# Pinning the VectorE instructions of the ten fast pairs to the order in which the kernel writes them

## The chip, the cores and the metric

One core of one Trainium2 chip runs the whole kernel. The metric is device time in microseconds, lower is better. The profile is one execution seen by the hardware profiler. TensorE is PE (its weight loads PEld), VectorE is DVE, ScalarE is ACT, GpSimd is POOL, SyncE is SP.

## The reference

A trunk of two layers is applied to a prompt (256 tokens) and a sample (512 tokens). Each layer has two SwiGLU blocks around a mixer:

```python
def swiglu_ffn(x, w_gate, w_up, w_down):
    return (jax.nn.silu(x @ w_gate) * (x @ w_up)) @ w_down
...
    def trunk(x):
        for l in range(DEPTH):
            x = layer_norm(ALPHA * x + 0.5 * swiglu_ffn(x, ffn1_w_gate[l], ffn1_w_up[l], ffn1_w_down[l]),
                           ln1_g[l], ln1_b[l])
            mix = hybrid_mixer(x, w_in[l], conv_w[l], conv_b[l], dt_bias[l], a_log[l], d_skip[l],
                               ssm_norm_g[l], attn_norm_g[l], rpb[l], w_out[l])
            x = layer_norm(ALPHA * x + mix, ln2_g[l], ln2_b[l])
            x = layer_norm(ALPHA * x + 0.5 * swiglu_ffn(x, ffn2_w_gate[l], ffn2_w_up[l], ffn2_w_down[l]),
                           ln3_g[l], ln3_b[l])
        return x
```

The model width is 1024, the inner width of the SwiGLU is 2816, and both groups together have 768 tokens. The four SwiGLU blocks are what this change touches.

## The kernel before

**Precision.** Every number is held as a high and a low part, and a product is three matmuls per contraction step: high by high, high by low of x, low by high. The high part of a weight block is a ScalarE cast. The low part is made in one of two ways (`parts`, L91). Without `acc`, VectorE subtracts (L106). With `acc`, ScalarE writes the negated high part (L102) and a DMA issued by GpSimd adds the raw weights onto it (L103); this is the *accumulate* below.

**Pairs and slots.** The inner width is worked off in eleven pairs of 256 columns. Pair 0 is plain. Pairs 1 to 10 are the *fast pairs* (`fast_pair`, L518): gate and up are each computed with seven block products in place of eight, so a pair has fourteen slots, numbered 0 to 13 (0 to 6 gate, 7 to 13 up). Slot i runs block product i (twelve matmuls of 384 columns, L524), and it uses *weight block* i, which is a raw quarter of the weights or a sum of quarters (L89, VectorE). Weight blocks are made four slots ahead, in five tiles `w0` to `w4` taken in turn, so that block i's tile is free again when product i-5 has ended. In pairs 2 to 9, blocks 0, 1, 5, 7 and 8 come by the accumulate.

**Down products.** The down projection of the pair before is spread over slots 1 to 11: three thirds of the tokens, each with seven products of three matmuls of 512 columns (L596) in the order h0, h1, h3, h4, h6, h5, h2 (names of the tiles of the hidden values; `h3h` is a high part, `h3l` a low part). h0, h4, h5, h2 of a third share a PSUM bank psB and h1, h3, h6 two banks psC. After each product VectorE adds the bank onto the result (L599), and the next product in that bank has to wait for it. At the end of a pair VectorE combines the four hidden blocks (L445 to L448) and makes h3l to h6l (L436).

**Down weights.** In slots 8 to 13 (`down_step`) the pair's own down weights are made: steps T1, T3 (slot 9), T2 (slot 11) and -T4 (slot 12) overwrite raw quarters on VectorE (L126, L128, L130, L132), and their high and low parts go to `w5` to `w11`. T2 in slot 11 yields `w8`, -T4 yields `w11`, both through the accumulate.

**Loads.** Raw weights come in halves of 512 KB on SP's queue (L71), six for each pair: gate, gate, up, up, down, down. There are four buffers `wraw`. A load is written into the program where a half is finished with (`done`), and its instruction waits on SP until the buffer that it was given is free.

**What sets the order.** When the program is built, a scheduler places each engine's instructions: an instruction may stand ahead of one that was written earlier on the same engine where the scheduler takes it as ready sooner, and a buffer is handed out in the order in which it takes buffers to come free. On the chip each engine then works its list from top to bottom.

## Time and profile before

| | |
|---|---|
| time, three runs | 2982.32 us median (2973.87 to 2982.59) |
| profiled execution | 2994.69 us, span 2992.5 us |
| PE busy | 2883.1 us (96% of the span) |
| PEld busy | 2534.0 us (85%) |
| DVE busy | 2191.0 us (73%) |
| ACT busy | 1583.4 us (53%) |
| POOL busy | 408.8 us (14%) |
| granted TensorE clock, mean | 0.978 of full speed |

Busy shares are means over the span. The fast pairs of the four SwiGLU blocks stand at 61.7 to 514.8, 1017.5 to 1466.9, 1556.0 to 2005.6 and 2506.0 to 2951.8 us. In each, the first, second and last pair are shaped differently from the seven in the middle (the first and the last have no down products, and the pair before the second has none), so the seven *middle pairs* of each block, 28 in all, are spoken of by themselves.

### The profile page before, as it was taken

To read this page: it belongs to the slowest core of one execution; us is meant where nothing else is said; L and a number is where in the kernel's file an instruction comes from. 1 tells how busy PE (TensorE), PEld (TensorE's weight loads), DVE (VectorE), ACT (ScalarE), POOL (GpSimd) and SP (SyncE) were. 2 spreads that over 40 slices of the span, in tenths; PEclk is the share of its full clock that TensorE was granted. 3 is DMA by queue.
4 is the path that set the end of the run, shared out by engine and by line. 5 is a ranking of instruction groups with operands and counts; after the bars stand their busy time and mean duration, and the time that the engine had idled before them with its cause. 6 is when DMAs were issued, how large, how long until landed. Compare 5 with 4: busy or idle time off the path is not lost.

```text
span 2992.5 us, 41957 instructions
## 1 busy us (share of the span) xinstructions
PE 2883.1 (96%) x15094; PEld 2534.0 (85%) x15094; DVE 2191.0 (73%) x4207; ACT 1583.4 (53%) x3231; POOL 408.8 (14%) x513
## 2 busy tenths in 40 slices
PE   8999999999999999999989999999999999999998
PEld 7988889888767888888979888898887778888897
DVE  7777777768435877777797778877783458887877
ACT  4645454657345455554545455545573464554543
POOL 2112120100000211121031121200000002121210
PEclk9999999999889999999999999999997999999999
DMA  3555453224323255554215554632343233454642
GB/s 122 126 121 126 114 127 114 99 88 137 111 62 125 81 134 110 128 128 112 85 36 122 125 126 114 140 100 102 99 124 114 76 122 92 113 132 109 135 106 77
DMA packets 128880, 330.26 MB, mean 110 GB/s; under 512 B 14816, under 2 KB 27296, under 8 KB 127904
## 3 DMA queue, kind: packets, MB, share of 16 engines
q1 hardware_dynamic: 82592, 243.68, 25.6%
q0 software_dynamic: 46080, 83.91, 16.4%
q8 instruction: 118, 1.93, 0.3%
q14 instruction: 90, 0.74, 0.1%
HBM read 224.67 MB, written 18.97 MB: 81 GB/s over the span
## 4 chain that ended last, share of the span: by engine, by line
PE 71%; DVE 11%; DMA 7%; issue 6%; POOL 3%; ACT 2%; POOLq 0%; DVEq 0%; SPq 0%; ACTq 0%
PE psA L524 28%; PE psB L596 7%; PE psA L1119 5%; PE psA L407 5%; PE psA L965 5%; PE psC L596 4%; DMA w<-wraw 4%; DMA wraw<-in_w_gu_dram 3%; PE psB L1054 3%; PE psB L618 3%; PE psC L618 3%; PE psA L772 2%; PE psA L992 2%; DVE arena L599 2%; PE psC L1083 2%
## 5 line engine op out<-in xcount | busy, mean ns | idle before, releaser
L524 PE MATMUL psA<-XH,w 128*128 128x384 f32 x2560 | 700.4, 338 | 5.3 <-DMA w<-wraw 5.3
L524 PEld LDWEIGHTS psA<-XH,w 128*128 128x128 f32 x2560 | 468.6, 188 | 14.4 <-DMA w<-wraw 6.6
L103 POOL DMA_DIRECT2D w<-wraw x320 | 273.8, 881 | 1322.9 <-ACT w L102 1168.0
L524 PE MATMUL psA<-XL,w 128*128 128x384 f32 x1280 | 432.6, 338 | 0.0
L105 ACT CAST w<-arena 128x512 fp32r<-128x512 f32 x320 | 198.4, 620 | 390.2 <-PE psA L524 357.4
L105 ACT CAST w<-wraw 128x512 fp32r<-128x512 f32 (+1 forms) x320 | 194.6, 620 | 214.4 <-PE psA L524 103.9
L106 DVE TENSOR_TENSOR w<-wraw,w 128x512 fp32r<-128x512 f32 (+1 forms) x320 | 216.0, 688 | 110.1 <-ACT w L105 106.3
L599 DVE SCALAR_TENSOR_TENSOR arena<-psB,arena 128x512 f32<-128x512 f32 x384 | 260.7, 686 | 45.5 <-PE psB L596 45.5
L106 DVE TENSOR_TENSOR w<-arena,w 128x512 fp32r<-128x512 f32 x320 | 219.6, 687 | 66.4 <-ACT w L105 66.4
L524 PEld LDWEIGHTS psA<-XL,w 128*128 128x128 f32 x1280 | 240.7, 188 | 7.5
L101 ACT CAST w<-wraw 128x512 fp32r<-128x512 f32 x320 | 197.4, 618 | 92.8 <-PE psA L524 56.5
L407 PE MATMUL psA<-XH,w 128*128 128x256 f32 (+1 forms) x1056 | 241.5, 335 | 5.0 <-DVE XH L372 5.0
L102 ACT ACTIVATE w<-w 128x512 fp32r<-128x512 f32 x320 | 198.8, 631 | 5.7
L599 DVE SCALAR_TENSOR_TENSOR arena<-psC,arena 128x512 f32<-128x512 f32 x288 | 191.7, 684 | 3.3
L407 PEld LDWEIGHTS psA<-XH,w 128*128 128x128 f32 x1056 | 168.6, 189 | 27.0 <-DVE XH L372 6.3
L524 PE MATMUL psA<-T4h,w 128*128 128x384 f32 x640 | 183.6, 348 | 0.0
L524 PE MATMUL psA<-T3h,w 128*128 128x384 f32 x640 | 181.1, 344 | 0.0
L524 PE MATMUL psA<-T2h,w 128*128 128x384 f32 x640 | 177.4, 338 | 0.0
L89 DVE TENSOR_TENSOR arena<-wraw 128x512 f32<-128x512 f32 x160 | 109.4, 686 | 91.9 <-DMA wraw<-in_w_gu_dram 81.6
L539 DVE TENSOR_TENSOR arena<-arena,psA 128x384 f32<-128x384 f32 x240 | 132.0, 550 | 56.9 <-PE psA L524 50.3
L330 POOL TENSOR_TENSOR stat<-stat,cst 128x1 f32<-128x1 f32 x60 | 25.7, 429 | 1033.2 <-ACT arena L933 415.7
L407 PE MATMUL psA<-XL,w 128*128 128x256 f32 (+1 forms) x528 | 151.1, 335 | 2.0 <-DVE XL L373 2.0
(359 smaller groups left out, 6356.0 us busy)
## 6 DMA issues: line engine op xcount, KB each, us to landing
wraw<-in_w_gu_dram SPq DMA_DIRECT2D x176, 512.0 KB, 3.8
w<-wraw POOLq DMA_DIRECT2D x320, 256.0 KB, 4.1
wraw<-in_w_dn_dram SPq DMA_DIRECT2D x88, 512.0 KB, 3.7
e<-ac_d SPq DMA_DIRECT2D x48, 256.0 KB, 3.3
wraw<-in_w_xbc_dram SPq DMA_DIRECT2D x16, 512.0 KB, 4.7
wraw<-in_w_qk_dram SPq DMA_DIRECT2D x16, 512.0 KB, 3.9
arena<-in_bias_dram SPq DMA_DIRECT2D x64, 128.0 KB, 2.1
wraw<-in_w_out_dram SPq DMA_DIRECT2D x16, 512.0 KB, 4.2
```

Source lines behind the costliest of these rows:

```text
L101: nc.scalar.copy(hi, raw)
L102: nc.scalar.activation(lo, hi.bitcast(F32), AF.Copy, scale=-1.0)
L103: nc.gpsimd.dma_start(lo, raw, accum_op=ALU.add)
L105: nc.scalar.copy(hi, raw)
L106: nc.vector.tensor_sub(lo, raw, hi.bitcast(F32))
L407: t_.matmul(ps[:, o : o + b - a], w[:, k % 4], xx[:, k, a:b], start=(k == 0 and part == 0 and i == 0), stop=(k == KD - 1 and part == 1))
L524: t_.matmul(ps, wx[:, k], xx[:, k], start=first and k == 0 and i == 0, stop=k == 3 and i == 2, skip_group_check=not first)
L596: t_.matmul(ps, hx, wx, start=first and k == 0, stop=k == 2, skip_group_check=not first)
L599: v_.scalar_tensor_tensor(sl, ps, 0.5, sl, op0=ALU.mult, op1=ALU.add)
L618: t_.matmul(ps[n], hx, units[2 * i + n][wx], start=(i == 0 and wi == 0), stop=(i == nf - 1 and wi == 2))
L965: t_.matmul(ps[r][:, : b - a], w[:, k % 4], xx[:, k, a:b], start=(k == 0 and part == 0 and i == 0), stop=(k == KD - 1 and part == 1))
L1119: t_.matmul(p[n], xx[:, k, cols], wo[2 * k + n][wx], start=(i == 0 and wi == 0), stop=(i == KD - 1 and wi == 2))
```

## The change

A small wrapper adds, to each VectorE instruction that it issues, an edge to the VectorE instruction written just before it. That pins the order and adds no wait on the chip. All VectorE instructions of pairs 1 to 10 go through it: the weight sums, the low parts, the down steps, the hidden blocks and the additions after down products. They are written slot by slot, within a slot in the order: weight block i+4, additions of block i's result, additions of two down products, down steps, hidden parts. No instruction is added or removed on any engine, and each computes what it did.

```diff
+class InOrder:
+    def __init__(self, tc, engine):
+        self.tc, self.engine = tc, engine
+
+    def __getattr__(self, name):
+        return lambda *a, **k: self.tc.keep_in_program_order(getattr(self.engine, name)(*a, **k))
...
-    def __init__(self, nc, pool, halves, units, temps, places):
+    def __init__(self, tc, pool, halves, units, temps, places):
+        nc, self.in_order = tc.nc, InOrder(tc, tc.nc.vector)
+        self.vector = nc.vector
...
-            (self.nc.vector.tensor_add if op == "add" else self.nc.vector.tensor_sub)(out, a, b)
+            (self.in_order.tensor_add if op == "add" else self.in_order.tensor_sub)(out, a, b)
...
-            nc.vector.tensor_sub(lo, raw, hi.bitcast(F32))
+            self.vector.tensor_sub(lo, raw, hi.bitcast(F32))
...
-        sub = self.nc.vector.tensor_sub
+        sub = self.vector.tensor_sub
...
+        ve = [nc.vector]
...
-                v_.tensor_sub(hs[i][1], src, hs[i][0].bitcast(F32))
+                ve[0].tensor_sub(hs[i][1], src, hs[i][0].bitcast(F32))
...
-            v_.tensor_add(a22, a21, a22)
+            ve[0].tensor_add(a22, a21, a22)
...
-                    v_.tensor_add(src, src, ps)
+                    ve[0].tensor_add(src, src, ps)
...
-                            v_.scalar_tensor_tensor(sl, ps, 0.5, sl, op0=ALU.mult, op1=ALU.add)
+                            ve[0].scalar_tensor_tensor(sl, ps, 0.5, sl, op0=ALU.mult, op1=ALU.add)
...
+        ve[0] = ws.vector = ws.in_order
         for p in range(1, NPAIR):
             fast_pair(p)
+        ve[0] = ws.vector = nc.vector
```

All pinned instructions carry L58, the wrapper's line, in the changed program, and later lines move by 10 to 13 (L101, L102, L105 become L113, L114, L117; L524 and L596 become L537 and L609). Three places of the built programs, all at the turn from one middle pair to the next of the second SwiGLU block, show how the rows stand.

The first is VectorE at the end of a pair. `wraw_10017` and `wraw_10036` are the two down halves, psB_10235 and psC_10262 banks of the last third, `wraw_10189` and `wraw_10215` the gate halves of the pair that follows. Before:

```order
L128 TENSOR_TENSOR wraw_10017<-wraw_10036,wraw_10017 128x512
L106 TENSOR_TENSOR w7_96<-wraw_10017,w7_96 128x512
L89 TENSOR_TENSOR arena_66<-wraw_10189,wraw_10215 128x512
L599 SCALAR_TENSOR_TENSOR arena_66<-psB_10235,arena_66 128x512
L130 TENSOR_TENSOR wraw_10017<-wraw_10036,wraw_10017 128x512
L599 SCALAR_TENSOR_TENSOR arena_66<-psC_10262,arena_66 128x512
L89 TENSOR_TENSOR arena_66<-arena_66,wraw_10189 128x512
L132 TENSOR_TENSOR wraw_10036<-wraw_10036,wraw_10017 128x512
```

The same place in the changed program:

```order
L58 TENSOR_TENSOR h0l_8103<-arena_66,h0h_8102 128x384
L58 SCALAR_TENSOR_TENSOR arena_66<-psB_10235,arena_66 128x512
L58 SCALAR_TENSOR_TENSOR arena_66<-psC_10262,arena_66 128x512
L58 TENSOR_TENSOR w7_96<-wraw_10017,w7_96 128x512
L58 TENSOR_TENSOR arena_66<-arena_66,psA_10274 128x384
L58 TENSOR_TENSOR arena_66<-arena_66 128x384
L58 SCALAR_TENSOR_TENSOR arena_66<-psB_10235,arena_66 128x512 x2
L58 TENSOR_TENSOR wraw_10017<-wraw_10036,wraw_10017 128x512
L58 TENSOR_TENSOR arena_66<-wraw_10189,wraw_10215 128x512
L58 TENSOR_TENSOR arena_66<-arena_66,wraw_10189 128x512
L58 TENSOR_TENSOR w0_89<-arena_66,w0_89 128x512
```

T2 (the row that writes `wraw_10017` from `wraw_10036`, L130 before) stood ahead of the last two additions from psB, those after h5 and h2 of the last third; now it stands behind both. -T4 (L132 before) stands four rows further down in the changed program, behind the addition after product 12.

The second is ScalarE after that turn. `wraw_10354` and `wraw_10379` are the up halves of the new pair, `w2_91` is block 4, `w0_89` block 7, `w1_90` block 8, `w11_100` the low and high part of -T4, and the COPY from psA_10393 that stands right ahead of `h3h` in the changed program is the one after product 2. Before:

```order
L105 CAST w2_91<-arena_66 128x512
L101 CAST w3_92<-wraw_10215 128x512
L534 COPY arena_66<-psA_10393 128x384
L102 ACTIVATE w3_92<-w3_92 128x512
L434 CAST h3h_8108<-arena_66 128x384
L105 CAST w4_93<-arena_66 128x512
L434 CAST h5h_8112<-arena_66 128x384
L434 CAST h4h_8110<-arena_66 128x384
L434 CAST h6h_8114<-arena_66 128x384
L101 CAST w0_89<-wraw_10354 128x512
```

The changed program there:

```order
L447 CAST h1h_8104<-arena_66 128x384
L113 CAST w11_100<-wraw_10036 128x512
L114 ACTIVATE w11_100<-w11_100 128x512
L547 COPY arena_66<-psA_10393 128x384
L447 CAST h3h_8108<-arena_66 128x384
L113 CAST w0_89<-wraw_10354 128x512
L447 CAST h5h_8112<-arena_66 128x384
L447 CAST h4h_8110<-arena_66 128x384
L447 CAST h6h_8114<-arena_66 128x384
L114 ACTIVATE w0_89<-w0_89 128x512
L113 CAST w1_90<-wraw_10379 128x512
L117 CAST w2_91<-arena_66 128x512
```

Block 4's high part stood ahead of the hidden parts and stands now behind the high parts of blocks 7 and 8, which read the up halves; block 7's stands in the middle of h3h to h6h.

The third is TensorE in slots 3 and 4 of the same pair (`T3h` is product 4, psA_10565 with `w0_89` product 7, psB_10433 the bank of the first third). Before:

```order
L524 MATMUL psA_10463<-XH_67,w1_90 128x384
L596 MATMUL psB_10433<-w8_97,h4h_8110 128x512 x2
L596 MATMUL psB_10433<-w8_97,h4l_8111 128x512
L596 MATMUL psC_10458<-w9_98,h6h_8114 128x512 x2
L596 MATMUL psC_10458<-w9_98,h6l_8115 128x512
L524 MATMUL psA_10393<-T3h_8123,w2_91 128x384
```

The changed program there:

```order
L609 MATMUL psC_10458<-w7_96,h3l_8109 128x512
L609 MATMUL psB_10530<-w5_94,h0h_8102 128x512 x2
L609 MATMUL psB_10530<-w5_94,h0l_8103 128x512
L537 MATMUL psA_10565<-XH_67,w0_89 128x384
L537 MATMUL psA_10565<-XL_68,w0_89 128x384
L537 MATMUL psA_10393<-T3h_8123,w2_91 128x384
L537 MATMUL psA_10393<-T3l_8124,w2_91 128x384
L537 MATMUL psA_10565<-XH_67,w0_89 128x384 x2
L537 MATMUL psA_10565<-XL_68,w0_89 128x384
L537 MATMUL psA_10393<-T3h_8123,w2_91 128x384 x2
```

h4 and h6 stood ahead of product 4 and stand behind it now, and five matmuls of product 7 have come up from slot 7. The first two use block 7's high part; the third (the first of "x2") is the first that uses its low part.

Lastly, the four buffers are handed out in another order, as the places of the tiles in the built programs show. In a middle pair before, the first up half takes the buffer of the same pair's first gate half, which the third sum (L89, gate's block 4) was the last to read, and the second up half takes that of the first down half of the pair before. In the changed program the first up half takes the buffer of the first down half of the pair before, whose last readers are the accumulate into `w8` (T2's) and -T4, and the second up half that of the second down half, whose last reader is the accumulate into `w11`.

## Rows read from the trace of the kernel before

**Rows 1.** Windows over the 28 middle pairs, one for each SwiGLU block, and sum

```profile
core 0: us, PE busy (x) PEld busy (x) DVE busy (x) ACT busy (x) POOL busy (x), PEclk, DMA share, GB/s
149.40:483.80 334.40, 320.14 (x1620) 290.30 (x1619) 260.15 (x454) 172.04 (x327) 54.65 (x64) 0.98 0.52 119
...
sum 1323.40, PE 1268.39 PEld 1152.48 DVE 1040.55 ACT 687.70 POOL 218.72; mean PE 317.10 PEld 288.12 DVE 260.14 ACT 171.92 POOL 54.68
```

**Rows 2.** Windows, the second fast pair of the second block (columns as above)

```profile
1059.60:1104.00 44.40, 44.40 (x232) 41.04 (x231) 37.49 (x66) 25.34 (x49) 7.71 (x9) 1.00 0.43 94
```

**Rows 3.** Waits of the whole span: us in total, times, longest us

```profile
DVE arena L89 <- DMA wraw<-in_w_gu_dram: 81.6, 28, 5.3
...
PE psB L596 <- DVE arena L599: 23.8, 32, 1.3
...
PE psC L596 <- DVE arena L599: 23.5, 28, 0.9
...
PEld psC L596 <- DVE h3l L436: 15.6, 17, 2.6
```

**Rows 4.** Timeline of SP, then DVE, at the turn to the pair starting 1198

```profile
1200.78 0.33 SPq L71 DMA_DIRECT2D wraw<-in_w_gu_dram  x1
...
1204.52 0.69 DVE L89 TENSOR_TENSOR arena<-wraw 128x512 f32<-128x512 f32 x1 [3.02 <-DMA wraw<-in_w_gu_dram]
1205.13 0.55 DVE L446 TENSOR_TENSOR arena<-arena 128x384 f32<-128x384 f32 x1
1205.60 0.55 DVE L436 TENSOR_TENSOR h3l<-arena,h3h 128x384 fp32r<-128x384 f32 x1
...
1208.88 0.69 DVE L599 SCALAR_TENSOR_TENSOR arena<-psB,arena 128x512 f32<-128x512 f32 x1
1209.48 0.68 DVE L106 TENSOR_TENSOR w<-arena,w 128x512 fp32r<-128x512 f32 x1
```

**Rows 5.** Timeline of PE in the same pair and just before it

```profile
1188.51 0.63 PE L596 MATMUL psC<-w,h6h 128*128 128x512 f32 x2
...
1189.21 0.34 PE L524 MATMUL psA<-T3h,w 128*128 128x384 f32 x1
...
1191.29 0.63 PE L596 MATMUL psB<-w,h5h 128*128 128x512 f32 x2
...
1209.71 0.70 PE L596 MATMUL psB<-w,h4h 128*128 128x512 f32 x2 [0.90 <-DVE arena L599]
...
1211.51 0.70 PE L596 MATMUL psC<-w,h6h 128*128 128x512 f32 x2 [0.86 <-DVE arena L599]
```

**Rows 6.** Timeline of ACT at the same turn

```profile
1201.02 0.63 ACT L102 ACTIVATE w<-w 128x512 fp32r<-128x512 f32 x1
...
1207.59 0.51 ACT L434 CAST h6h<-arena 128x384 fp32r<-128x384 f32 x1 [0.42 <-DVE arena L448]
1208.01 0.62 ACT L101 CAST w<-wraw 128x512 fp32r<-128x512 f32 x1
```

**Rows 7.** Timeline of POOL at the same turn: issues of accumulates

```profile
1194.23 0.86 POOL L103 DMA_DIRECT2D w<-wraw  x1 [1.22 <-ACT w L102]
...
1201.95 0.86 POOL L103 DMA_DIRECT2D w<-wraw  x1 [2.90 <-ACT w L102]
```

**Rows 8.** Accumulates by tile w, issue to landing

```profile
DMA to landing us min/median/max: 3.2/4.1/8.0
```

**Rows 9.** Weight loads by line L71, issue to landing

```profile
DMA to landing us min/median/max: 3.4/3.8/10.6
```

**Rows 10.** Line L524: for what its engine sat idle, us and times

```profile
  DMA w<-wraw: 11.9, 8
```

**Rows 11.** Windows around PE's waits: PE busy second, PEclk third from the end

```profile
1111.00:1118.00 7.00, 5.25 (x26) 4.06 (x25) 7.00 (x15) 4.58 (x9) 1.47 (x2) 1.00 0.57 150
...
1592.00:1596.40 4.40, 2.00 (x12) 1.68 (x11) 2.27 (x4) 1.51 (x3) 0.85 (x1) 1.00 0.80 158
1596.40:1599.80 3.40, 3.40 (x13) 3.40 (x12) 0.00 (x0) 0.18 (x1) 0.00 (x0) 0.51 0.45 149
```

More of the change, by code (lines that the diff above doesn't have):

```diff
@@ L278, in trunk @@
     wt = [pers.tile([P, 2 * ZN], F32R, name=f"w{i}") for i in range(NW)]
-    ws = WeightStream(nc, wpool, halves, units, [at(o_sum + i * UNIT, UNIT) for i in range(3)], wt)
+    ws = WeightStream(tc, wpool, halves, units, [at(o_sum + i * UNIT, UNIT) for i in range(3)], wt)
     y = at(o_y, NT * DM).rearrange("p (t d) -> p t d", t=NT)
@@ L444, in finish @@
                 return
-            v_.tensor_add(a22, a21, a22)
-            v_.tensor_sub(a21, a11, a21)
-            v_.tensor_sub(a11, a22, a11)
-            v_.tensor_sub(a12, a12, a11)
+            ve[0].tensor_add(a22, a21, a22)
+            ve[0].tensor_sub(a21, a11, a21)
+            ve[0].tensor_sub(a11, a22, a11)
+            ve[0].tensor_sub(a12, a12, a11)
             put_h((3, a22), (4, a11), (5, a21), (6, a12))
@@ L542, in block @@
                 else:
-                    v_.tensor_mul(sg[:, i, h], sg[:, i, h], src)
+                    ve[0].tensor_mul(sg[:, i, h], sg[:, i, h], src)
             units_ = down_units(p - 1) if p - 1 in dnw else []
```

## The prediction

> **What bounds the kernel now.** I read the windows of the 28 middle pairs first. They take 1323.4 us, 47.26 each, and PE is busy for 1268.4 of that [rows 1]. A second pair of a block that nothing disturbs takes 44.40 us with PE busy throughout [rows 2]. So PE's own work is 44.4 us a pair, 2.86 us of each middle pair (80 us in all) are lost, and that is the most that any better order could give back there. DVE is busy for 1040.55/28 = 37.2 us a pair [rows 1], ACT and POOL for less: only PE is a bound, and a new order costs or gains what it makes PE wait.
>
> The waits say where the 2.86 us go [rows 3]: PE waits for VectorE's additions from psB and psC (47.3 us in all) and for h3l (15.6 us), and VectorE waits, once in each of 28 pairs and 81.6 us in all, in a weight sum (L89) for a load. The timeline joins them [rows 4]: the second up half is issued at 1200.78, the sum stands in VectorE's list ahead of L446 and h3l, so these and the additions from psB and psC behind them come 3.02 us late, and PE then waits 0.90 and 0.86 us before h4 and h6 [rows 5]. The sum is for blocks 9 and 10, wanted in slots 9 and 10; it has merely been placed early.
>
> **The change, part by part.** No instruction is added, so all costs are waits.
>
> *The early sum.* Written in slot 5, it now stands behind h3l to h6l and the first additions. VectorE's 81.6 us of waiting go, and with them what PE waits for h3l and the additions; in the changed PE order h4 and h6 also come a product later. This is worth up to 2.86 us a pair.
>
> *T2, the buffers and the up halves.* In the same move T2 goes behind the additions after h5 and h2 of the last third, and the buffer of the first up half becomes the one that T2's accumulate reads. I follow this from 0, the end of the last matmul of the pair before. Prices: twelve matmuls of a product 2.08 us (0.175 each) and three of a down product 0.70 [rows 5]; VectorE 0.60 a step for 512 columns and 0.47 for 384 [rows 4]; ACT 0.42 a hidden part, 0.62 a weight cast, 0.63 a negated copy, and 0.3 from its end to POOL's issue [rows 6, 7]; an accumulate 4.1 us to landing (3.2 to 8.0) [rows 8], a load 3.8 (3.4 to 10.6) [rows 9].
>
> - h2 of the last third is followed by ten matmuls of product 13, so it ends at -1.75 plus some 0.15 of tail: -1.6. Its addition, then T2: done at -0.3.
> - ACT casts T2's high part to 0.35, casts block 3 in between, writes the negated copy to 1.5; POOL issues at 1.8; the accumulate lands at 5.9. Then SP starts the first up half, landing 9.8.
> - -T4 follows T2 by two sums, a low part, an addition (0.6, 0.6, 0.6 and 0.47, with a wait for ACT): done at 3.9. ACT casts it, negates it to 5.1, POOL issues at 5.4, landing 9.5; the second up half lands at 13.4.
> - ACT is through with the copy after product 2 and h3h at 7.4, and then stands at block 7's cast, which reads the first up half, until 9.8. Cast, h5h, h4h, h6h and negated copy end at 12.3, POOL issues at 12.6, block 7's low part lands at 16.7. ACT has meanwhile gone to block 8's cast, which waits for the second up half until 13.4; block 4's cast behind it ends at 14.6.
> - PE from 0 does seven matmuls of product 0, products 1 to 3, h0, h1, h3 and the next third's h0: 1.2 + 3 x 2.08 + 4 x 0.70 = 10.3, then two of product 7. At 10.65 it wants block 4's high part and gets it at 14.6 (wait 4.0). Two matmuls on, at 15.0, it wants block 7's low part and gets it at 16.7 (wait 1.7). Together **5.7 us a pair**.
>
> From the shortest landings (3.2 and 3.4) the same sum gives: first up half 8.5, block 7's low part 14.5, so 3.5 us. From a long one (the accumulate issued at 1194.23 is the last reader of the buffer whose load starts at 1200.78, so 6.5 us [rows 7, 4]) it gives 21.5 and 10.5 us. I take 6.2, near the medians, and 0.5 above them because the three accumulates and two loads now run beside each other more than before. The Trainium skill (DMA: Bandwidth & Descriptors, Anatomy of one DMA — SWDGE path) puts a GpSimd-issued transfer at about 2.0 us plus bytes over 436 GB/s; for 256 KB that is an estimate of 2.6 us. By it and 3.2 us for 512 KB the two waits would come to about 2.1 us and the kernel would gain slightly. The trace disagrees: the shortest of all accumulates is 3.2 us.
>
> *The clock.* PE waited 2.4 us in the stretch 1592 to 1596.4, and the granted clock then stood at half for 3.4 us; two waits of under 0.9 us in 1111 to 1118 did not lower it [rows 11]. A wait of 4.0 us in each pair should do so nearly every time: 3.4 us at half speed cost 1.7, times 0.9 is 1.5 us a pair.
>
> *The rest of the pair.* Behind the stall VectorE has caught up, and the additions that PE wants in turn (h0, h3, h4, ...) stand in the order of their products, so I add nothing there. VectorE idles more, since it waits at each addition for its product, but has 44.4 - 37.2 = 7 us to spare. First, second and last pairs get no stall of this kind: their up halves don't hang on a T2 behind additions, or need no accumulate. At the end of three blocks the table of scales (`load_gb`) now stands ahead of the next weights on SP. They come some 12 us later, at most, in front of 18 to 38 us of down products and normalization, so nothing; without that cover 12 us each, 36 in all.
>
> Sum: a middle pair takes 44.4 + 6.2 + 1.5 = 52.1 us against 47.26, so 28 x 4.84 = 136 us. The profiled execution took 2994.7 us: 3130. The median of the runs shown is 0.41% below that execution, and so I predict **3117 us**.
>
> **Rivals.**
> 1. *The transfers land early, and the gain is kept (faster).* The stall shrinks with each landing; below 2.86 us without a lowered clock the change wins. At a stall of 1 us a pair takes 45.4: 28 x 1.86 = 52 us less, 2930 us; with none at all 44.4, 2903 us. For it: VectorE's 3.02 us wait really goes. Against: it needs every accumulate and load below the shortest of 320 and of 328 seen [rows 8, 9]. The page's rule above is this case. Chance 0.07.
> 2. *The one stall takes the other's place (no change).* A stall of about 2.9 us and no lowered clock give 2980 us. It needs the shortest landings and a weaker cover than I read; chance 0.05.
> 3. *Short landings, clock kept.* 44.4 + 3.5 = 47.9: 18 us more, 3000 us. Together with what lies between it and my sum it is part of the forecast's range.
> 4. *Transfers get in each other's way.* Accumulates and loads share the DMA engines, whoever issues them, says the Trainium skill (DMA: Bandwidth & Descriptors, Issuing engines are not separate DMA queues); the 6.5 us above agree. With a stall of 8 us and the clock lowered for twice as long (3.4 us) a pair takes 55.8: 239 us more, 3221 us. Chance of that and above 0.10.
>
> That the order would not change is excluded by the rows of the built program.
>
> **How the numbers follow.** Forecast 0.78 (3.5 to 8 us of stall), rival 1 0.07, rival 2 0.05, rival 4 0.10. Range: 3000 (the shortest landings, clock kept) to 3215 (just below rival 4); what falls outside is rivals 1, 2 and 4, about 2 in 10. Some 0.3% is what a measurement can tell from no change: slower 0.88, same 0.05, faster 0.07.
>
> **What would show it.** In the changed profile: VectorE's wait in the sums for gate/up loads falls from 81.6 us to under 20. PE's waits for additions and h3l fall from 63 us to under 25. New: PE in front of T3's product waits for ACT's cast of block 4 (some 28 x 4 us; weight loads may carry the wait), and in product 7 for an accumulate into w (28 x 1 to 2 us, where it was 11.9 us in 8 waits [rows 10]). ACT waits in a cast (L113) for a gate/up load, some 28 times 2 us and more. The clock of the blocks falls below 0.98. I would be wrong if the first up half were issued before 3 us into the pair, if PE found block 4 and block 7 there on time, or if the early additions still came late.

## The result, and the profile after

The changed kernel takes 3147.82 us (median of 4 runs, 3141.34 to 3182.75) against 2978.1 us in the same comparison: ratio 1.0607, 95% interval 1.0515 to 1.0699. It is slower, as forecast; the forecast was 3117 us. Its profiled execution took 3150.1 us. The page's first lines:

```profile
span 3148.1 us, 41671 instructions
...
PE 2899.7 (92%) x15094; PEld 2561.1 (81%) x15094; DVE 2213.9 (70%) x4207; ACT 1592.2 (51%) x3231; POOL 408.2 (13%) x513
```

The windows over the 28 middle pairs, columns as in [rows 1]:

```profile
152.16:527.99 375.83, 328.97 (x1618) 299.25 (x1618) 265.50 (x453) 175.09 (x327) 55.31 (x65) 0.92 0.47 105
...
sum 1504.89, PE 1320.47 PEld 1202.63 DVE 1061.93 ACT 700.17 POOL 221.25; mean PE 330.12 PEld 300.66 DVE 265.48 ACT 175.04 POOL 55.31
```

A middle pair takes 1504.89/28 = 53.75 us, where it took 47.26 [rows 1]. PE idles for (1504.89 - 1320.47)/28 = 6.59 us of it and is busy for 47.16, which is 2.76 more than in the undisturbed 44.40 [rows 2]: the granted clock is 0.92, where [rows 2] have 1.00, and the same matmuls take longer. The waits that changed, in the form of [rows 3]:

```profile
DVE w L58 <- ACT w L117: 210.1, 176, 5.5
...
DVE arena L58 <- PE psB L609: 189.5, 92, 4.7
...
ACT w L113 <- DMA wraw<-in_w_gu_dram: 175.5, 78, 5.0
...
PE psA L537 <- ACT w L117: 137.6, 28, 6.1
...
PE psA L537 <- DMA w<-wraw: 44.3, 27, 2.9
...
PE psA L537 <- ACT arena L547: 11.4, 7, 3.4
```

VectorE's wait in a weight sum for a load and PE's waits for additions and h3l, the rows of [rows 3], have left the list. Two new PE waits stand there: 137.6 us for a cast on ScalarE, once in each of 28 middle pairs, and 44.3 us for an accumulate. The chain of waits that ends at the second of them, in the pair that starts at 1240.36, is the predicted loop in one view:

```profile
1243.05 3.27 DMA w<-wraw
...
1246.35 0.03 SPq L83
...
1246.47 4.58 DMA wraw<-in_w_gu_dram
...
1251.07 0.62 ACT w L113
1251.69 0.41 ACT h5h L447
...
1252.93 0.54 ACT w L114
...
1253.76 6.89 DMA w<-wraw
...
1260.69 1.33 PE psA L537 x3
```

From top to bottom: w8's accumulate, the first up half that SP holds back for it, the cast of block 7, the hidden parts and the negated copy, block 7's accumulate, and PE in product 7. The timeline of the same turn shows PE's two waits, then T2, -T4, h4l and the sum of block 4 on VectorE, what ScalarE waits for, and the issue of w11's accumulate:

```profile
1239.25 0.39 PE L609 MATMUL psB<-w,h2l 128*128 128x512 f32 x1
...
1257.38 0.69 PE L537 MATMUL psA<-T3h,w 128*128 128x384 f32 x1 [5.02 <-ACT w L117]
1257.87 0.53 PE L537 MATMUL psA<-T3l,w 128*128 128x384 f32 x1
1260.69 1.01 PE L537 MATMUL psA<-XH,w 128*128 128x384 f32 x2 [2.29 <-DMA w<-wraw]
...
1240.29 0.68 DVE L58 TENSOR_TENSOR wraw<-wraw 128x512 f32<-128x512 f32 x1
...
1244.38 0.69 DVE L58 TENSOR_TENSOR wraw<-wraw 128x512 f32<-128x512 f32 x1
...
1252.55 0.56 DVE L58 TENSOR_TENSOR h4l<-arena,h4h 128x384 fp32r<-128x384 f32 x1 [2.06 <-ACT h4h L447]
...
1253.96 0.68 DVE L58 TENSOR_TENSOR arena<-wraw 128x512 f32<-128x512 f32 x1
...
1256.20 0.62 ACT L113 CAST w<-wraw 128x512 fp32r<-128x512 f32 x1 [2.73 <-DMA wraw<-in_w_gu_dram]
1256.72 0.61 ACT L117 CAST w<-arena 128x512 fp32r<-128x512 f32 x1
...
1246.71 0.86 POOL L115 DMA_DIRECT2D w<-wraw  x1 [0.75 <-ACT w L114]
```

ScalarE waits 2.73 us in the cast of block 8 for the second up half; block 4's cast stands right behind, and PE starts product 4 when it is through.

That is one of two reasons why block 4 is late. PE came to product 4 at 1252.36 (1257.38 - 5.02), and at that time block 4's sum had not been made. In the written order it stands on VectorE behind h4l to h6l; h4l waited 2.06 us for h4h, and h4h stands on ScalarE behind block 7's cast, which waited for the first up half. The sum ended at 1254.65. Had ScalarE cast it at once (0.6 us), PE would still have waited 2.9 us; the other 2.1 are those behind block 8's cast. The medians over the 28 middle pairs say the same: the sum ends 2.3 us after PE's wish, and its cast starts 2.0 us after that.

The clock in windows of that pair (third number from the end):

```profile
1247.00:1252.00 5.00, 5.00 (x26) 4.15 (x25) 3.32 (x7) 1.93 (x4) 0.57 (x1) 1.00 0.91 191
1252.00:1255.00 3.00, 0.36 (x2) 0.04 (x1) 2.10 (x4) 1.46 (x4) 0.84 (x1) 0.90 0.45 147
1255.00:1258.00 3.00, 0.61 (x2) 0.50 (x2) 0.64 (x2) 1.67 (x3) 0.00 (x0) 0.50 0.96 210
...
1261.00:1264.00 3.00, 3.00 (x10) 3.00 (x10) 0.52 (x1) 0.00 (x0) 0.00 (x0) 0.50 0.84 205
```

It falls to 0.50, the lower of its two levels (1.2 GHz), during the first wait and is still there when PE works again.

The middle pairs cost 1504.89 - 1323.40 = 181.5 us more, the two executions lie only 155.4 apart. The four second pairs take 193.3 us and took 180.1, 13.2 more, which the prediction did not see. In the timeline of one (ScalarE, PE) the cast of block 8 waits for the second up half, and the copy of a bank that PE needs stands behind it:

```profile
1097.71 0.62 ACT L113 CAST w<-wraw 128x512 fp32r<-128x512 f32 x1 [3.50 <-DMA wraw<-in_w_gu_dram]
...
1099.83 0.46 ACT L547 COPY arena<-psA 128x384 f32<-128x384 f32 x1
...
1100.34 0.44 PE L537 MATMUL psA<-T4h,w 128*128 128x384 f32 x1 [2.54 <-ACT arena L547]
```

On the other side the two mixers, which the change does not touch, took 36.5 us less; windows over them, before and then after:

```profile
514.50:1017.50 503.00, 493.37 (x2648) 401.70 (x2648) 318.63 (x748) 274.48 (x634) 37.75 (x60) 0.95 0.31 100
2005.20:2506.00 500.80, 491.01 (x2650) 400.05 (x2649) 318.77 (x749) 274.81 (x635) 37.77 (x60) 0.96 0.31 102
```

```profile
558.35:1041.80 483.45, 473.26 (x2651) 389.03 (x2651) 321.68 (x755) 275.73 (x638) 37.98 (x60) 1.00 0.33 107
2127.20:2611.10 483.90, 473.08 (x2650) 389.09 (x2650) 321.78 (x755) 276.56 (x639) 37.64 (x60) 1.00 0.33 108
```

The profile of before holds a stretch of 44 us in the one mixer and one of 41 us in the other at half clock, that of after none. 181.5 + 13.2 - 36.5 = 158.2; the remaining -2.8 us are spread over the rest.

### The profile page after: what moved, and what is told of

Its sections match the earlier page's. It is cut to its first block, busy times and chain, and to the rows that moved or that the text cites. A ratio compares the mean times of both kernels' runs of the same rounds, so it can differ in the third digit from the quotient of the medians.

```text
span 3148.1 us, 41671 instructions
## 1 busy us (share of the span) xinstructions
PE 2899.7 (92%) x15094; PEld 2561.1 (81%) x15094; DVE 2213.9 (70%) x4207; ACT 1592.2 (51%) x3231; POOL 408.2 (13%) x513
## 3 DMA queue, kind: packets, MB, share of 16 engines
q0 software_dynamic: 46080, 83.91, 15.7%
## 4 chain that ended last, share of the span: by engine, by line
PE 68%; DMA 14%; DVE 6%; ACT 6%; issue 5%; POOL 1%; SPq 0%; POOLq 0%; DVEq 0%; ACTq 0%
PE psA L537 27%; DMA w<-wraw 8%; PE psB L609 7%; DMA wraw<-in_w_gu_dram 6%; PE psC L609 5%; PE psA L419 5%; PE psA L980 4%; PE psA L1134 4%; PE psB L631 2%; PE psA L787 2%; PE psC L631 2%; PE psB L1069 2%; PE psA L1007 2%; PE psC L1098 2%; ACT w L113 1%
## 5 line engine op out<-in xcount | busy, mean ns | idle before, releaser
L537 PE MATMUL psA<-XH,w 128*128 128x384 f32 x2560 | 710.3, 344 | 49.7 <-DMA w<-wraw 44.3
L537 PEld LDWEIGHTS psA<-XH,w 128*128 128x128 f32 x2560 | 472.6, 190 | 87.3 <-DMA w<-wraw 58.3
L537 PE MATMUL psA<-XL,w 128*128 128x384 f32 x1280 | 436.4, 341 | 0.0
L58 DVE SCALAR_TENSOR_TENSOR arena<-psB,arena 128x512 f32<-128x512 f32 x384 | 260.0, 684 | 189.6 <-PE psB L609 189.5
L58 DVE TENSOR_TENSOR w<-arena,w 128x512 fp32r<-128x512 f32 x312 | 214.5, 688 | 203.3 <-ACT w L117 203.3
L537 PE MATMUL psA<-T3h,w 128*128 128x384 f32 x640 | 214.9, 400 | 137.6 <-ACT w L117 137.6
L113 ACT CAST w<-wraw 128x512 fp32r<-128x512 f32 x320 | 197.0, 619 | 261.9 <-DMA wraw<-in_w_gu_dram 175.5
L117 ACT CAST w<-arena 128x512 fp32r<-128x512 f32 x320 | 197.6, 618 | 208.4 <-DVE arena L58 204.5
L117 ACT CAST w<-wraw 128x512 fp32r<-128x512 f32 (+1 forms) x320 | 193.7, 621 | 193.6 <-PE psA L537 96.0
L537 PEld LDWEIGHTS psA<-T3h,w 128*128 128x128 f32 x640 | 145.8, 232 | 150.0 <-ACT w L117 146.5
L537 PEld LDWEIGHTS psA<-XL,w 128*128 128x128 f32 x1280 | 243.9, 191 | 5.9
L58 DVE SCALAR_TENSOR_TENSOR arena<-psC,arena 128x512 f32<-128x512 f32 x288 | 191.9, 684 | 51.2 <-PE psC L609 47.1
L547 ACT COPY arena<-psA 128x384 f32<-128x384 f32 x240 | 113.8, 474 | 180.8 <-PE psA L537 180.7
L114 ACT ACTIVATE w<-w 128x512 fp32r<-128x512 f32 x320 | 200.3, 630 | 5.3
L537 PE MATMUL psA<-T4h,w 128*128 128x384 f32 x640 | 185.2, 350 | 11.6 <-ACT arena L547 11.4
L537 PE MATMUL psA<-T2h,w 128*128 128x384 f32 x640 | 177.4, 338 | 0.0
L58 DVE TENSOR_TENSOR arena<-arena,psA 128x384 f32<-128x384 f32 x280 | 153.2, 547 | 30.3 <-ACT arena L547 24.0
```

Source lines behind the costliest of these rows:

```text
L58: return lambda *a, **k: self.tc.keep_in_program_order(getattr(self.engine, name)(*a, **k))
L113: nc.scalar.copy(hi, raw)
L114: nc.scalar.activation(lo, hi.bitcast(F32), AF.Copy, scale=-1.0)
L117: nc.scalar.copy(hi, raw)
L537: t_.matmul(ps, wx[:, k], xx[:, k], start=first and k == 0 and i == 0, stop=k == 3 and i == 2, skip_group_check=not first)
L547: s_.copy(t, banks[m, 1])
```

## The experiments

Two theories stood against each other at first. Mine: T2 and -T4 late, so the down halves' buffers late, so the up halves, ScalarE's casts and PE. The rival: a pinned VectorE waits in order, and that is the price. The table gives each run's median with its ratio to the kernel before, the mean of its middle pairs, and from its trace the medians over these 28 pairs, in us from the pair's start: T2 and -T4 of the pair before done, the two up halves landed, block 4's cast done, PE's wish for it (the end of what PE did just before product 4), and PE's wait there. A pair starts where the 168 matmuls of products in the pair before have been counted on PE. That lies 4.9 us ahead of product 2 in every kernel but e8 (5.6); in the changed kernel five matmuls of product 0 already stand ahead of it, so it lies 0.88 us before the zero of the prediction.

| kernel | us | ratio, interval | pair | T2 | -T4 | up 1 | up 2 | cast 4 | wish | wait |
|---|---|---|---|---|---|---|---|---|---|---|
| before | 2978 | 1 | 47.26 | -7.2 | -4.8 | 1.2 | 6.4 | 0.8 | 14.3 | 0 |
| changed | 3147.82 | 1.0607 | 53.75 | 0.6 | 4.7 | 10.7 | 15.7 | 16.9 | 12.0 | 4.9 |
| e1 | 2912.99 | 0.9787 (0.9743 to 0.9831) | 44.52 | -8.2 | -4.8 | 4.7 | 7.3 | 7.2 | 11.9 | 0 |
| e2 | 2885.61 | 0.9698 (0.9647 to 0.9748) | 44.50 | -5.5 | -0.3 | 6.4 | 11.2 | 8.2 | 10.5 | 0 |
| e3 | 3095.2 | 1.0373 (1.0305 to 1.0442) | 51.37 | -3.5 | 4.5 | 9.1 | 16.3 | 17.5 | 11.9 | 5.7 |
| e4 | 2924.02 | 0.9823 (0.9781 to 0.9866) | 45.95 | -0.6 | 4.2 | 11.3 | 13.5 | 12.3 | 11.6 | 0.8 |
| e5 | 3008.57 | 1.0114 (1.0049 to 1.0179) | 47.90 | -1.5 | 2.6 | 8.2 | 13.1 | 14.3 | 12.1 | 2.2 |
| e6 | 2922.76 | 0.984 (0.9771 to 0.9909) | 46.00 | -1.5 | 0.8 | 8.7 | 11.6 | 11.7 | 13.2 | 0 |
| e7 | 2863.83 | 0.9626 (0.9568 to 0.9685) | 44.28 | -0.8 | 0.3 | -0.6 | 9.2 | 1.8 | 11.9 | 0 |
| e8 | 3111.07 | 1.0445 (1.0377 to 1.0514) | 51.29 | -2.2 | -1.5 | 9.5 | 14.3 | 19.5 | 18.5 | 0.9 |
| e9 | 3025.11 | 1.0182 (1.0112 to 1.0252) | 49.85 | 0.6 | 1.3 | 10.2 | 13.1 | 15.2 | 14.4 | 0.9 |
| e10 | 3077.33 | 1.0342 (1.0273 to 1.041) | 51.14 | 0.6 | 4.7 | 10.7 | 15.6 | 16.8 | 12.0 | 4.9 |
| e11 | 2941.58 | 0.9893 (0.9828 to 0.9958) | 46.20 | -1.5 | 0.8 | 8.7 | 11.5 | 12.7 | 13.1 | 0 |
| e12 | 2911.75 | 0.9766 (0.9695 to 0.9838) | 45.45 | -5.0 | -4.2 | 11.1 | 13.2 | 11.8 | 11.5 | 0.4 |

Pairs are the surer measure: a mixer with such a half-clock stretch makes a single execution some 20 us longer.

**e1: only the sums pinned.**

```diff
-        ve[0] = ws.vector = ws.in_order
...
-        ve[0] = ws.vector = nc.vector
```

> Only the weight sums (L101 of the changed kernel) are pinned; low parts, down steps, hidden parts and additions are left to the scheduler. In the built program the first sum over the up halves stands behind h6l, as in the changed kernel, T2 stands ahead of the last third's last two additions, block 4's cast stands ahead of block 7's, and h4 and h6 ahead of product 4, as in the kernel before. The up halves go into the down halves' buffers, as in the changed kernel. My theory (T2 late, so the up halves late, so ScalarE's casts late): T2 and w8's accumulate some 4 us earlier, first up half landing about 5 to 6 us into the pair, no wait for block 4; VectorE's 81.6 us of waiting in the sums under 20; middle pairs 44.6 to 45.5 us, 2900 to 2935 us in all, so faster than the kernel before. Rival, that the down halves' buffers alone make the loads too late wherever T2 stands: middle pairs 49 us and more, 3030 us and more. Rival, that the early sum's wait was worth nothing: 2978 us, no change.

As my theory had it. The pair of 44.52 us is [rows 2]'s: the early sum's wait was worth the 2.7 us a pair that the prediction put on it, and the down halves' buffers do no harm by themselves.

**e2: the down steps free.**

```diff
-        sub = self.vector.tensor_sub
+        sub = self.nc.vector.tensor_sub
```

> The changed kernel with only the down steps T1, T3, T2, -T4 free again. T2 goes to right behind the low part of w7, ahead of four additions and two sums; -T4 stays behind them; block 4's cast is then ahead of block 8's and behind block 7's; the buffers are as in the changed kernel. My theory: T2 is done about 4 us earlier, first up half lands about 6 us into the pair, block 7's cast is through by 9 and block 4's by 9.6, before PE wants it at 10.7: middle pairs 44.6 to 46, 2905 to 2945 us. Rival, that VectorE waits in order at additions and casts (189.5 us for psB, 210.1 us for casts in the changed kernel) and this is what costs: these waits stay, and with them 3100 us and more.

Faster than I expected, since the pair is the undisturbed one. All else on VectorE is pinned, and its waits are still there:

```profile
DVE w L58 <- ACT w L117: 133.0, 143, 2.6
...
DVE arena L58 <- PE psB L609: 58.4, 89, 1.5
```

191 us of waiting in order, where the changed kernel had 400, and PE loses nothing by them. As the price of the whole change the rival falls; e4, with VectorE wholly pinned, shows the small part of it that holds.

**e3: T2 written in slot 10.**

```diff
-        STEPS = {8: (0,), 9: (1, "T1", "T3"), 10: (2,), 11: ("T2", 3, 4), 12: ("-T4", 5), 13: (6,)}
+        STEPS = {8: (0,), 9: (1, "T1", "T3"), 10: (2, "T2"), 11: (3, 4), 12: ("-T4", 5), 13: (6,)}
```

> The changed kernel, still wholly pinned, with one word moved: T2 is written at the end of slot 10 and not at the start of slot 11's steps, so it stands right behind w7's low part and ahead of the addition after product 11 and the last two additions from psB. -T4 stays; ScalarE's list keeps block 7's cast ahead of h5h and block 8's cast ahead of block 4's. My theory: the first up half comes about 4 us earlier, so block 7's low part is in time (the 44.3 us of PE waits for w<-wraw go), but block 4's cast still stands behind block 8's, which waits for the second up half, whose chain starts at -T4: of the 137.6 us for block 4 most stays. Middle pairs 50 to 52.5, 3045 to 3110 us. Rival, that T2's place alone makes the loss: middle pairs 44.6 to 46, 2905 to 2945 us.

The time is in my range and block 4's wait stays, but two links are not as I had them. PE's waits for accumulates fell from 44.3 to 16.1 us and did not go, and T2 came 4.1 us earlier, the first up half only 1.6. In all 28 pairs its load is issued 0.07 to 0.10 us after the end of -T4, which reads T2's result, is the other last reader of that buffer, and was left where it stood. The turn to the pair that starts at 1257.10:

```profile
1260.90 0.68 DVE L58 TENSOR_TENSOR wraw<-wraw 128x512 f32<-128x512 f32 x1
...
1261.66 7.68 SPq L83 DMA_DIRECT2D wraw<-in_w_gu_dram  x2
```

**e4: ScalarE's casts in written order.** VectorE stays wholly pinned. Each weight cast and negated copy gets an edge to the one written before it.

```diff
-            nc.scalar.copy(hi, raw)
+            self.scalar.copy(hi, raw)
...
+        ws.scalar = ws.casts
         for p in range(1, NPAIR):
             fast_pair(p)
+        ws.scalar = nc.scalar
```

> The changed kernel with VectorE pinned as it is, T2 as late and the same buffers, and ScalarE's weight casts and negated copies of pairs 1 to 10 chained to each other in the order in which they are written (blocks 4, 5, 6, then 7, then 8). PE then has product 4 and two matmuls of product 7 before h4, and the rest of product 7 after product 6. My theory, by its last link: the up halves land as late as in the changed kernel (first about 10.7, second about 15.9 us into the pair), but block 4's cast no longer stands behind them, so PE's waits for block 4 (137.6 us) go and block 7's low part is wanted some 8 us later: middle pairs 44.6 to 47, 2905 to 2975 us. Rival, that late loads make PE wait whatever stands in front of ScalarE's list: the wait moves to products 7 and 8, middle pairs 50 us and more, 3040 us and more.

The up halves land as late as in the changed kernel, or nearly (11.3 and 13.5 us), and the loss is gone: 25.3 us of idle PE in 28 pairs are left of 184. Late halves alone are no loss. What makes them one is what stands behind their casts on ScalarE, and that PE's list holds product 7 early (both lists moved here; e10 takes the second apart). What is left is not the halves' either. In the pair that starts at 1208.97, block 4's cast waits for its sum, which VectorE makes behind h6l:

```profile
1220.62 0.62 ACT L68 CAST w<-arena 128x512 fp32r<-128x512 f32 x1 [1.97 <-DVE arena L58]
```

PE's wait for it is 0.8 us (median of the 28 pairs). That much the pinned order of VectorE costs by itself, and it is what holds of the rival.

**e5: the additions free.** The bracket with "336 of 512 columns" in the expectation is a slip; 168 additions of 512 columns in each block are meant.

```diff
-                            ve[0].scalar_tensor_tensor(sl, ps, 0.5, sl, op0=ALU.mult, op1=ALU.add)
+                            v_.scalar_tensor_tensor(sl, ps, 0.5, sl, op0=ALU.mult, op1=ALU.add)
```

> The changed kernel with the additions after down products (336 of 512 columns from psB and psC in each block) free again; sums, low parts, down steps and hidden parts stay pinned. In the built program the scheduler still puts both last additions from psB ahead of T2, so T2 is as late, block 4's cast still stands behind block 8's, but product 7's early matmuls are gone: PE has h4 and two matmuls of product 4, h6, and then the rest of product 4. My theory: one wait a pair, for block 4, whose cast ends some 16 us into the pair: about 4.6 us, and 1.7 to 2.5 us for the clock; middle pairs 50 to 51.5 us, 3035 to 3110 us. Rival, that the additions' pinned places and VectorE's 189.5 us of waiting for psB in them are the cause: middle pairs 44.5 to 46, 2885 to 2945 us.

Between the two and below my range: the one wait is there, but 2.2 us and not 4.6, since all steps came 2 us earlier in the pair (T2 at -1.5, -T4 at 2.6), which I had taken as unmoved. The additions are a part of the lateness, not the whole.

**e6: e1 with T2 pinned.**

```diff
-            sub(b11, b22, b11)
+            self.in_order.tensor_sub(b11, b22, b11)
```

> The kernel of e1 (only the sums pinned, 2913 us, middle pairs 44.5) with one more instruction pinned in each pair: T2, which so goes behind the last two additions from psB as in the changed kernel. The buffers are those of the changed kernel (up halves into the down halves' buffers), PE's order is that of the kernel before, block 4's cast stands behind block 7's alone. My theory: the first up half lands 10 to 10.7 us into the pair as in the changed kernel; h6's high part and block 4's cast behind block 7's end by 11.8 and 14; PE wants h6 at 11.1 and block 4 at about 12: 1 to 3 us of waits, middle pairs 45.5 to 48, 2940 to 3010 us. Rival, that T2's place alone carries the whole loss: 52 us and more, 3120 us and more. Rival, that it costs nothing once ScalarE's and PE's orders are sound: 2913 us.

The pair is as expected (46.00), the time below the range because I had set out from e1's 2913 us. The profile of e1 has one of the long half-clock stretches in a mixer (500.1 us in place of 481.5), and its four first pairs take 195.4 us, where those of e6 take 168.0. A late T2, in the buffers of the changed kernel but with PE's order of before and block 4's cast behind block 7's alone, costs 1.48 us a pair (46.00 - 44.52). PE pays it ahead of h6 and not for block 4:

```profile
PE psC L609 <- DVE arena L612: 33.5, 27, 2.9
```

h6's high part stands behind block 7's cast on ScalarE, and the additions that PE waits for stand behind its low part on VectorE.

**e7: the kernel before with T2 alone pinned.** The edit of e6, in the kernel before; all else that the change pins is free.

```diff
-            sub(b11, b22, b11)
+            self.in_order.tensor_sub(b11, b22, b11)
```

> The kernel before with T2 alone pinned. T2 stands behind the last two additions from psB as in the changed kernel, but the four buffers are handed out as in the kernel before: the first up half goes into the first gate half's buffer, the second into that of the first down half, which w8's accumulate reads last. The sum over the up halves has moved behind h6l in this program too; block 4's cast stands behind blocks 7's and 8's. My theory, by its buffer link: the first up half is not late at all, the second lands 10 to 10.7 us into the pair, block 4's cast ends at about 12.3 where PE wants it at about 12: middle pairs 44.6 to 46.5, 2890 to 2965 us. Rival, that a late T2 costs what the changed kernel loses whatever the buffers: 50 us and more, 3055 us and more.

This is the fastest kernel of the study, 3.7% below the one before and 9% below the changed one, by one edge in each pair with down steps. The expectation misread one thing: block 4's cast is early here (done at 1.8), as in the kernel before. T2 is 6.4 us later than before and nobody waits for it, since the first up half has another buffer; the sum over the up halves has moved behind h6l, and its wait is gone (2.9 us are left). Between the two profiled executions lie 130.8 us, 83.6 of them in the middle pairs; 40 are in the mixers, where e7 has no half-clock stretch, and the edit is no shown cause of that. The sum of the windows over the middle pairs:

```profile
sum 1239.74, PE 1239.74 PEld 1152.28 DVE 1043.04 ACT 699.58 POOL 221.72; mean PE 309.94 PEld 288.07 DVE 260.76 ACT 174.90 POOL 55.43
```

PE is busy in all of it.

**e8: T2 and -T4 in slot 10, all pinned.**

```diff
-        STEPS = {8: (0,), 9: (1, "T1", "T3"), 10: (2,), 11: ("T2", 3, 4), 12: ("-T4", 5), 13: (6,)}
+        STEPS = {8: (0,), 9: (1, "T1", "T3"), 10: (2, "T2", 3, "-T4"), 11: (4,), 12: (5,), 13: (6,)}
```

> The changed kernel, wholly pinned, with T2 and -T4 written one behind the other at the end of slot 10, right behind the low part of w7 (w8's parts with them; w9's stay in slot 11), ahead of the additions of slots 11 and 12 and of slot 12's sums. ScalarE still has block 4's cast behind block 8's. My theory, both chains early: T2 is done at about -4 and -T4 at about -3.4; w11's cast still waits behind h2h until -1, its accumulate lands at about 4.5, and the second up half at about 9 (15.7 in the changed kernel), block 4's cast ends by 11.5, where PE wants it at about 12: middle pairs 44.5 to 46, 2885 to 2945 us. Rival, that a pinned VectorE costs time wherever the steps stand: 49 us and more, 3015 us and more.

A clear miss, by 166 us. The timeline of the turn to the pair that starts at 1271.26 (VectorE, ScalarE, POOL, SP):

```profile
1266.91 1.42 DVE L58 TENSOR_TENSOR wraw<-wraw 128x512 f32<-128x512 f32 x2
...
1269.53 0.62 ACT L113 CAST w<-wraw 128x512 fp32r<-128x512 f32 x1 [2.66 <-PE psB L609]
...
1270.72 1.18 ACT L113 CAST w<-wraw 128x512 fp32r<-128x512 f32 x2
...
1272.73 1.74 POOL L115 DMA_DIRECT2D w<-wraw  x2 [0.78 <-ACT w L114]
...
1276.19 6.29 SPq L83 DMA_DIRECT2D wraw<-in_w_gu_dram  x2
```

T2 and -T4 are done at 1268.3, but w10's cast stands in ScalarE's list ahead of w8's, and waits until h5 of the last third has used w10. w8's accumulate is issued at 1272.7, 1.5 us after the pair's start, and the first up half at 4.9, little sooner than in the changed kernel (median 6.1). PE's waits for accumulates come to 87.2 us. The step of this expectation that failed is that the first chain starts at T2. It starts where ScalarE casts T2's result, and in e3 at -T4.

**e9: -T4 alone moved up.**

```diff
-        STEPS = {8: (0,), 9: (1, "T1", "T3"), 10: (2,), 11: ("T2", 3, 4), 12: ("-T4", 5), 13: (6,)}
+        STEPS = {8: (0,), 9: (1, "T1", "T3"), 10: (2,), 11: ("T2", 3, 4, "-T4"), 12: (5,), 13: (6,)}
```

> The changed kernel, wholly pinned, with -T4 alone moved up: to the end of slot 11, right behind T2 and ahead of slot 12's sums and low part. T2 stays behind the last two additions from psB. ScalarE's list then has block 7's cast ahead of h3h, block 8's behind h6h and block 4's behind block 8's; PE has product 7's early matmuls ahead of product 4 as in the changed kernel. My theory, two chains: the second up half comes some 3 us earlier (12 to 13 us into the pair), but the first still lands at 10.7, now in front of h3h, and block 7's low part at 18 to 19: the wait for block 4 turns into waits for h3 and for block 7's low part. Middle pairs 50 to 54 us, 3040 to 3155 us. Rival, that the second chain alone (137.6 of the 182 us of waiting) makes the loss: 45 to 48 us, 2905 to 2990 us.

The waits went where my theory sent them, at a smaller price (49.85 us a pair and 3025 us in all, both just below their ranges):

```profile
PE psC L609 <- ACT h3h L447: 61.3, 28, 3.0
...
PE psA L537 <- DMA w<-wraw: 21.0, 29, 1.4
...
PE psA L537 <- ACT w L117: 18.3, 19, 1.5
```

With the second chain shortened, the first takes over: block 7's cast now stands ahead of h3h and waits for the first up half.

**e10: block 7's low part by VectorE.**

```diff
-                        acc = not isinstance(x, str) and 1 < p < NPAIR - 1 and (m, x) != (1, 3)
+                        acc = not isinstance(x, str) and 1 < p < NPAIR - 1 and (m, x) not in ((1, 3), (1, 0))
```

> The changed kernel with block 7's low part made by VectorE's subtraction and not by an accumulate (block 8 keeps its accumulate). ScalarE still has block 4's cast behind block 8's; PE has two matmuls of product 7, then product 4 in one piece, and product 7's low part much later. My theory: the first wait a pair stays (about 4.5 us, for block 4), the second, for block 7's accumulate (44.3 us in all), goes, and with it part of the half-clock time (8.5 us a middle pair): middle pairs 50 to 51.7 us, 3040 to 3095 us. Rival, that block 7's low part only takes its place in PE's queue and another wait follows: 53 us and more, 3125 us and more.

As expected, and a second reading of the clock: the sum of the windows over the middle pairs, and the wait that is left.

```profile
sum 1431.95, PE 1294.33 PEld 1185.24 DVE 1082.14 ACT 686.30 POOL 197.19; mean PE 323.58 PEld 296.31 DVE 270.53 ACT 171.58 POOL 49.30
```

```profile
PE psA L537 <- ACT w L117: 137.2, 35, 5.2
```

4.92 us of waiting a pair ((1431.95 - 1294.33)/28), nearly all of it this one wait, go with 1294.33/28 - 44.40 = 1.83 us more of PE's work. Two waits of 6.59 us went with 2.76. The clock rows over the 28 pairs give 4.14 us a pair at half clock here, 0.79 of them inside waits, and 8.53 and 3.52 in the changed kernel. At half speed the rest costs 1.7 and 2.5 us.

**e11: e6 with block 4's cast behind block 8's.** One edge on ScalarE in each middle pair.

```diff
+            if u.get("role") == (0, "S3"):
+                self.b4 = self.cast
+            elif u.get("role") == (1, 1):
+                self.tc.add_manual_dep(self.b4.ins, self.cast.ins.name, mybir.DependencyInfo(
+                    mybir.DependencyClass.NoSync, mybir.DependencyReason.DATA), reason="late")
```

> The kernel of e6 (sums and T2 pinned, 2923 us, middle pairs 46.0) with one edge more in each middle pair: block 4's cast is put behind block 8's in ScalarE's list, as in the changed kernel. PE's order is nearly unchanged (h4 and h6 ahead of product 4). My theory: ScalarE's order costs only as far as the second up half is late. In e6 that half lands at 11.6 us into the pair, since -T4 is done at 0.8 and not at 4.7; block 4's cast would end at about 12.8, and PE wants it at 13.2: 0 to 0.5 us a pair, 2915 to 2945 us. Rival, that standing behind the casts of the up halves is itself the loss: 4 us and more a pair, 3035 us and more.

0.2 us a pair, as expected. ScalarE's list alone is no loss either, if -T4 is not late and block 4's sum is early (here it ends 2.1 us ahead of PE's wish, in the changed kernel 2.3 us behind it).

**e12: e8 with the casts of e4.**

```diff
-        STEPS = {8: (0,), 9: (1, "T1", "T3"), 10: (2,), 11: ("T2", 3, 4), 12: ("-T4", 5), 13: (6,)}
+        STEPS = {8: (0,), 9: (1, "T1", "T3"), 10: (2, "T2", 3, "-T4"), 11: (4,), 12: (5,), 13: (6,)}
...
+        ws.scalar = ws.casts
```

> The kernel of e8 (wholly pinned, T2 and -T4 at the end of slot 10; 3111 us, against expectation) with ScalarE's weight casts and negated copies chained in the order in which they are written, as in e4. In e8 the cast of w8 stands behind that of w10, which waits for the product h5 of the last third, so w8's accumulate started no earlier than in the changed kernel although T2 was done 3 us earlier. Here w8's cast stands ahead of w9's and w10's, and block 4's ahead of those of blocks 5, 7 and 8. Theory: it was ScalarE's list that kept e8 slow: first up half landing at about 5 us, block 4 and block 7 in time as in e4, with e4's 1 us of wait for block 4 left (its sum stands behind h6l): middle pairs 44.8 to 46.2, 2890 to 2945 us. Rival, that the early down steps themselves cost (VectorE or the transfers): 49 us and more, 3015 us and more.

The time is as expected, the reason only half: block 4 is in time, but the first up half lands at 11.1 us and not at 5. Its buffer is now released by w10's accumulate, which reads the other quarter of the same half and is issued after w8's (in the pair that starts at 1207.37 at 1211.26; the load follows at 1214.68). So e12 shows once more that late halves cost little when block 4 does not stand behind them.

## Why the prediction was right

The direction, the chain of loads and the place were right. Two terms were too small, two were missing, and one of two paths by which block 4 comes late was overlooked. That 3130 came within 20 us of the profiled execution is in part luck.

- *The early sum.* VectorE's wait for the load and PE's for additions and h3l went, as forecast. e1 and e7 show that this is worth 2.7 to 3.0 us a pair.
- *The chain from T2.* In the pair that starts at 1240.36 the prediction's zero is 1241.24 (h2 ends at 1239.64). Predicted and measured: T2 done -0.3 and -0.27, w8's accumulate issued 1.8 and 1.8, landed 5.9 and 5.1, first up half landed 9.8 and 9.8, -T4 done 3.9 and 3.8, w11's accumulate issued 5.4 and 5.5, second up half landed 13.4 and 14.9, block 4's cast 14.6 and 16.1, block 7's low part landed 16.7 and 19.4. PE's waits there: 4.0 and 5.02, 1.7 and 2.29.
- *Block 4's sum.* The prediction takes it as ready and puts VectorE's order behind the stall at nothing. The sum stands behind h6l, ended a median 2.3 us after PE's wish, and by itself made 2.9 of the 4.9 us; block 8's cast, the one reason that the prediction names, made the other 2.0. The wait came out near the forecast because both paths hang on the late up halves.
- *The stall.* 6.2 us forecast, 6.59 measured. In this pair rival 4 had the lengthened transfers right in kind: 6.89 us for the accumulate that ran beside two loads, 3.27 for the first of the chain. The 6.5 us that the prediction read before are 6.4 to the landing; the load behind it was released 0.1 us later by a ScalarE cast.
- *The clock* was the mis-sized term: 1.5 us forecast for one lowered stretch a pair, where PE's work grew by 2.76. The clock stands at half for 8.5 us of a middle pair (sum of its rows over 28), 3.5 of them inside the waits, where they cost nothing; the other 5.0 cost 2.5 us at half speed. The remaining 0.3 need not be the clock: in e4 PE is busy for 45.05 us a pair at a clock of 1.00, 0.65 above [rows 2]. By the difference to e10 the second wait carries 0.93 of the 2.76.
- *Second pairs* were put at nothing and cost 13.2 us. *The mixers* were taken at their own profiled time, which held two long half-clock stretches; without them the base is 36.5 us lower. 44.4 + 6.59 + 2.76 = 53.75, so 28 x 1.65 = 46 us more than forecast for the middle pairs, + 13 - 36.5 - 3: the execution came out 20 us above the 3130 forecast for it. Misses of +46 and +13 us met one of -36.5; that they nearly cancel is luck. The other 11 of the 31 us between 3117 and 3147.82 come from the 0.41% taken off for the median.

Rival 1, short landings, fell. The accumulates of the changed kernel by tile w, issue to landing:

```profile
DMA to landing us min/median/max: 3.2/3.7/8.6
```

An estimate for them by the rule of the Trainium skill (DMA: Bandwidth & Descriptors, Anatomy of one DMA — SWDGE path), 2.6 us, is again below the shortest.

What the experiments add to the argument: no single link carries the loss. A late T2 costs nothing in other buffers (e7) and 1.5 us in these (e6); with ScalarE's casts in written order a pair stays 1.1 to 1.6 us above 44.40 although both halves are late (e4, e12), and PE's idle part of that (0.9 and 0.5 us) is mostly its wait for block 4's sum; block 4 behind block 8 costs 0.2 us where the second half is in time (e11). Late up halves, hidden parts and block 4 behind their casts on ScalarE, block 4's sum behind those hidden parts on VectorE, and PE with product 7 early make 9.35 us together. The page "PSUM — Partial Sum Buffer" of the Trainium skill (Engine vs sequencer instructions) calls ScalarE's queue strictly first in, first out. The trace agrees: block 4's sum ended at 1254.65, and its cast started at 1256.72, behind block 8's, which had waited for a load until 1256.20.

Two things stay open. An edge on VectorE also moves what the scheduler does on ScalarE and PE, so that e2, e5, e8 and e9 each changed several lists, and the edges on ScalarE in e4 and e12 moved PE's; only e11 isolates one. No run moves block 4's sum alone. And the clock was not tested apart from the waits that lower it.

## What to carry to other kernels

Pinning one engine's order re-orders the others: read every engine's list and the buffers after such a change, above all the in-order engine between the loads and the bound one. Pin the single instruction whose place costs something (here T2, or the sums) and not the whole engine: middle pairs of 44.28 us (e7) against 53.75. A late transfer costs only what stands behind it in some list, so look for ready work that is queued behind a waiting instruction.

## What the runs showed of the hardware that was not expected

In the profile of before the granted clock stood at 0.50 in the mixers for 44.30 and 40.90 us at a stretch, while PE was busy for 44.26 and 40.90 of them. Of the other thirteen profiles, eight hold no such stretch, four one, and e8 one of 41 and one of 58 us. A mixer takes 481 to 485 us without one, 500 to 504 with one of 41 to 44 us, and 511 with the one of 58. Nothing in the profile says why: ahead of the one at 794.3 PE idles 1.04 and 1.01 us, and e7 has the same two gaps at that place with the clock at 1.00 throughout. A wait of 4.9 us in each pair went with 1.8 us more of PE's work (e10).
